# Normalising attention probabilities inside their transposing product

## The chip, the cores and the metric

The kernel runs on one core of a Trainium2 chip. The metric is the device time of one execution in microseconds; the time of the kernel before is the median of three runs. Each engine of the core (TensorE, here PE; VectorE, DVE; ScalarE, ACT; GpSimd, POOL; SyncE, SP) works through its own queue in order, and they wait for each other through semaphores. PEld is TensorE's loading of weights, which is recorded apart from its products. The rows come from one profiled execution.

## The reference

Two layers of a hybrid block over 512 latent tokens and 256 context tokens, 1024 wide. Each layer has a neighbourhood attention, a state-space mixer (SSD) and a grouped-query attention side by side, then a feed-forward part. The change touches only the softmax that both attentions use:

```python
def gqa_softmax_attention(q, k, v):
    s = jnp.einsum('bqgrd,bkgd->bgrqk', q, k) * (HEAD_DIM ** -0.5)
    p = jax.nn.softmax(s.astype(jnp.float32), axis=-1).astype(v.dtype)
    return jnp.einsum('bgrqk,bkgd->bqgrd', p, v)
```

Everything is float32. The neighbourhood attention has the same form, with a bias and a window mask added to `s`.

## The kernel before

The large projections (`proj_ws`, its product is L348, and `proj_as`, L362) split each float32 operand into a high and a low part of the type fp32r and add three products. They fill most of the span. The attention of a layer is a stage of its own between the input projections and the output projection: about 270 to 430 us in layer 0 and 1250 to 1385 us in layer 1.

Attention is cut into units. One unit is one head `j` of a pair, one block of 128 queries `qi`, and the 256, 640 or 768 keys that these queries see (2, 5 or 6 tiles of 128). Layer 0 has 48 units, layer 1 has 32; together they have 384 tiles. A unit goes through four steps:

- `scores` (L402, L405): two fp32r products into the PSUM tile `S`; DVE adds a bias where there is one and takes the row maximum (L410, L414, L415, or L419, L420); ACT writes the exponentials to the SBUF tile `pr` and, by the accumulator, their row sums (L422). Queries lie on the partitions, keys along the row.
- `normalise` (L426, L427): DVE takes the reciprocals of the 128 sums, then POOL multiplies the whole of `pr` by them, in place.
- `transposes` (L436): for each tile of 128 keys TensorE transposes 128x128 of `pr` into the PSUM tile `PT`, three tiles to a `PT`, and ACT (L440) or DVE (L442) copies them to `PHA` or `PHB`.
- `values` (L448): after both heads, TensorE multiplies the transposed probabilities by the values; both heads run side by side in the two halves of the array.

The loop that issues them (at the end of the mixer part) is software-pipelined by hand: in turn `i` it issues the scores of unit `i + 2`, then `normalise` of unit `i + 1`, then `transposes` of unit `i`, then `values` of the unit before. Between them a list of events with due times (`U = UCFG[l]`, L1101, and the lines behind it) spreads the work of the SSD mixer over the units: `diag` (row broadcasts by DMA; ACT L912 and L918; DVE L916, L923, L924, L931, L932, L940; POOL L927; TensorE L921, L937, L938), `steps` (POOL L963 and L1003; TensorE L982 and L995; DVE L977, L990, L1000), `skip` (POOL L944) and `gate` (DVE L1027, POOL L280). The biases of the neighbourhood attention are made on POOL too (L613). So in this stage all engines carry attention and mixer in one stream each.

The kernel is written on a layer that sets all waits and chooses tile buffers. It is called with a planner (`schedule_with_timeline_sim`, L1405), which sets the order of the instructions on each engine from the order of the program and its own estimate of their times. Tiles with one tag share a number of buffers: `pr` has three; `zt` has two of 128x256 floats and is used, ahead of attention, by the gate of the mixer (L810 to L814: two DVE or ACT steps, then a store to DRAM).

Of the kernel before, what the change touches and what calls it, by code (L numbers as in the profile page):

```python
# [11 lines left out]
ALU = mybir.AluOpType  # L12
AX = mybir.AxisListType

P = 128
# [13 lines left out]
def hybrid_kernel(ctx: ExitStack, tc: tile.TileContext, a, out, dbg=None):  # L29
# [4 lines left out]
    sb = ctx.enter_context(tc.tile_pool(name="sb", bufs=1))  # L34
# [5 lines left out]
    def nm(s):  # L40
        uid[0] += 1
        return f"{s}_{uid[0]}"

    def T(pool, tag, bufs, shape, dt=F32):
        return pool.tile(shape, dt, tag=tag, bufs=bufs, name=nm(tag))
# [7 lines left out]
    def slot(tag, dt=F32, shape=(P, NT)):  # L53
        return T(sb, tag, BUFS[tag], list(shape), dt)
# [16 lines left out]
    def tiny(n):  # L71
        if n <= 16:
            return T(sb, "tiny", 14, [P, n])
        return T(sb, "tiny36", 5, [P, n]) if n <= 36 else T(sb, "tiny96", 4, [P, n])

    def ps_s():
        return T(ps, "S", 2, [P, 1024])

    def ps_t():
        return T(ps, "PT", 2, [P, 512])  # L80

    def ps_sm():
        return T(ps, "sm", 2, [P, 512])
# [28 lines left out]
    V = nc.vector  # L112
    S = nc.scalar
    G = nc.gpsimd
    PE = nc.tensor
# [5 lines left out]
    ident = c0[:, 0:P]  # L121
# [265 lines left out]
    def attn(V2, xk, kts, qcols, bias, yout):  # L387


        nkt = len(kts)  # L390
        nk = nkt * P
        ng = (nkt + 2) // 3
        o0 = 512 - (xk[1] - xk[0]) if xk else 512
        ph, pr, t2, ms = {}, {}, {}, {}

        def scores(qk, j, qi):
            Q, K1, K2 = qk()
            q0 = qcols[qi]
            st = ps_s()
            for i, K in enumerate((K1, K2)):  # L400
                if xk:
                    PE.matmul(  # L402
                        st[:, o0:512], lhsT=Q[:, q0 : q0 + P], rhs=K[:, xk[0] : xk[1]], start=(i == 0), stop=(i == 1)
                    )
                PE.matmul(st[:, 512:768], lhsT=Q[:, q0 : q0 + P], rhs=K[:, 512:768], start=(i == 0), stop=(i == 1))  # L405
            m = ms[j, qi] = tiny(8)
            if bias is not None:
                if j not in t2:
                    t2[j] = bias(j)
                V.tensor_tensor_reduce(  # L410
                    out=st[:, o0:512], in0=st[:, o0:512], in1=t2[j][qi], scale=1.0, scalar=-3.0e38,
                    op0=ALU.add, op1=ALU.max, accum_out=m[:, 0:1],
                )
                V.tensor_reduce(out=m[:, 1:2], in_=st[:, 512:768], op=ALU.max, axis=AX.X)  # L414
                V.tensor_scalar(  # L415
                    out=m[:, 2:3], in0=m[:, 0:1], scalar1=m[:, 1:2], scalar2=-1.0, op0=ALU.max, op1=ALU.mult
                )
            else:
                V.tensor_reduce(out=m[:, 0:1], in_=st[:, o0:768], op=ALU.max, axis=AX.X)  # L419
                V.tensor_scalar_mul(m[:, 2:3], m[:, 0:1], -1.0)  # L420
            p_ = pr[j, qi] = T(sb, "pr", 3, [P, nk])
            exps.append(S.activation(p_, st[:, o0:768], AF.Exp, bias=m[:, 2:3], accum_out=m[:, 3:4]).ins)  # L422

        def normalise(j, qi):
            m, p_ = ms[j, qi], pr[j, qi]
            V.reciprocal(m[:, 4:5], m[:, 3:4])  # L426
            G.tensor_scalar(out=p_, in0=p_, scalar1=m[:, 4:5], scalar2=1.0, op0=ALU.mult, op1=ALU.mult)  # L427

        def transposes(j, qi):
            t_ = ph[j, qi] = slot("PH" + "AB"[j], F32, (P, 6, P))  # L430
            for i in range(ng):
                n = min(3, nkt - 3 * i)
                pt = ps_t()
                for k in range(n):
                    kk = 3 * i + k
                    PE.transpose(pt[:, k * P : (k + 1) * P], pr[j, qi][:, kk * P : (kk + 1) * P], ident)  # L436
                ptv = pt[:, 0 : n * P].rearrange("p (k q) -> p k q", q=P)
                dst = t_[:, 3 * i : 3 * i + n, :]
                if i % 2 == 0 or qi:
                    S.activation(dst, ptv, AF.Copy)  # L440
                else:
                    V.tensor_copy(dst, ptv)  # L442

        def values(qi):
            pv = ps_sm()
            for k in range(nkt):
                for j in range(2):
                    PE.matmul(  # L448
                        pv[64 * j : 64 * j + 64, 0:P], lhsT=V2(kts[k], j), rhs=ph[j, qi][:, k, :],
                        start=(k == 0), stop=(k == nkt - 1), tile_position=(0, 64 * j),  # L450
                    )
            yout(pv, qi)

        return [
            (lambda qk, j=j, qi=qi: scores(qk, j, qi), lambda j=j, qi=qi: normalise(j, qi),
             lambda j=j, qi=qi: transposes(j, qi), (lambda qi=qi: values(qi)) if j else None, j,
             (lambda j=j: t2.update({j: bias(j)})) if bias is not None and qi == 0 else None)
            for j in range(2) for qi in range(2)
        ]
# [46 lines left out]
    for l in range(L):  # L506
# [63 lines left out]
        for i in range(2, 4):  # L570
            step_md(4)
            w = wblk(i)
            pt = ps_s()
# [10 lines left out]
        for b in range(2):  # L584
            step_md(4)
            w = wv[b]
            pt = ps_s()
# [8 lines left out]
            for i in range(2):  # L596
                pt = ps_t()
# [20 lines left out]
        def na_sets():  # L618
            for b in range(2):
# [7 lines left out]
                for half in range(nhalf):  # L627
                    yt = []

                    def yout(pv, qi, b=b, half=half, yt=yt):  # L630
                        if qi == 0:
                            yt.append(sb_())
                        yv = yt[0]
                        if half < 2:
                            yv = yv.rearrange("p (r c) -> p r c", r=8)
                            ov = yv.rearrange("p r c -> p c r")[:, 16 * qi : 16 * qi + 16, :]
                            S.activation(ov, pv[:, 0:P].rearrange("p (c r) -> p c r", r=8), AF.Copy)
                            ydst = ydr[b][:, 0:512].rearrange("p (r c) -> p r c", c=64)[:, :, 32 * half : 32 * half + 32]
                        else:
                            S.activation(yv[:, qi * P : qi * P + P], pv[:, 0:P], AF.Copy)  # L640
                            ydst = ydr[b][:, 512:768]
                        if qi == 1:
                            nc.scalar.dma_start(ydst, yv)

                    if half < 2:
                        units += attn(
                            vsel, (128 * half, 128 * half + 384), [half, half + 1, half + 2, 4, 5],
                            [256 * half, 256 * half + 128], lambda j, b=b, half=half: na_bias(2 * b + j, half), yout,
                        )
                    else:  # L650
                        units += attn(vsel, None, [4, 5], [512, 640], None, yout)
# [72 lines left out]
        def gqa_sets():  # L724
            for g in range(2):
                def prep(g=g):
                    kk = prep_k(gqk[0], 64 * g)
                    return [(prep_q(gqk[1 + g], 64 * j, ntok), *kk) for j in range(2)]

                def vsel(kt, j, g=g):  # L730
                    return Vg[:, kt, 64 * g : 64 * g + 64]

                units = []
                for half in range(nhalf):
                    def yout(pv, qi, g=g, half=half):
                        k = 6 + g
                        if yh[k] is None:
                            yh[k], yl[k] = (mb([P, NT], F32R) if g else slot("GV", F32R) for _ in range(2))
                        o = 256 * half + P * qi
                        split(yh[k][:, o : o + P], yl[k][:, o : o + P], pv[:, 0:P])  # L740

                    if half < 2:
                        units += attn(vsel, (0, 512), list(range(6)), [256 * half, 256 * half + 128], None, yout)
                    else:
                        units += attn(vsel, None, [4, 5], [512, 640], None, yout)
                yield prep, units
# [261 lines left out]
        zt = []  # L1008
# [212 lines left out]
        for i, d in enumerate(dA):  # L1221
            events(nu + i)
            w = load_wo(d, 0)
            pt = ps_s()
# [5 lines left out]
        for d in range(KB - 2):  # L1230
            w = load_wo(d)
            pt = ps_s()
# [43 lines left out]
        for gi, ng in enumerate(groups):  # L1276
# [34 lines left out]
            for d in range(KB - 2 if fin else KB):  # L1311
                w = load_dn(d)
                pt = ps_s()
# [95 lines left out]
```

## Time and profile before

| | |
|---|---|
| median of 3 runs | 1808.84 us (1803.02 to 1810.6) |
| profiled execution | 1808.68 us, of which its span is 1806.9 us |
| TensorE busy | 1727.2 us (96%) |
| DVE busy | 1072.8 us (59%) |
| POOL busy | 395.0 us (22%) |
| mean granted TensorE clock | 0.978 of 2.4 GHz |

An engine's busy time is the union of its instructions' spans. TensorE's products overlap, and a product's recorded span includes the time that it takes to run out; so in a row of equal products the distance from start to start, not the duration of one, is what another product costs. The chain of waits follows the work that ended last back through what released it. Idle time is shown with the instruction that ended it.

### The profile page before, as it was taken

The page shows a single profiled execution, that of the slowest core. Times are in us where ns is not written, and L with a number is a line of the kernel's source. Part 1 is how long each engine was busy: PE and PEld are TensorE (multiplying, and loading weights), DVE is VectorE, ACT ScalarE, POOL GpSimd, SP SyncE. Part 2 cuts the span into 40 slices and gives each one's busy share as a digit, 9 for nine tenths or more (in the row PEclk, how much of TensorE's full clock was granted, in tenths as well). Part 3 has the DMA queues.
Part 4 walks back from the last instruction along what each step waited for, and adds up shares of the span by engine and source line. Part 5 has one row for each costly group of instructions (what it writes and reads, how often), then busy time and mean ns, then how long its engine had stood idle before and what let it go on. Part 6 is the DMA issues. An engine that isn't in the chain of part 4 may idle for free.

```text
span 1806.9 us, 26557 instructions
## 1 busy us (share of the span) xinstructions
PE 1727.2 (96%) x10146; PEld 1472.2 (81%) x10146; DVE 1072.8 (59%) x2141; ACT 682.5 (38%) x1376; POOL 395.0 (22%) x385
## 2 busy tenths in 40 slices
PE   7997798999999999999999999999899999999998
PEld 3887697777888888888888878988777888888887
DVE  4749957986575464445644576586886733333335
ACT  4564665665252211221122224333565532222222
POOL 0398876652010000000000001222652100000000
PEclk9999898999989999999999999999999999999999
DMA  9653474622224343334343445233622333333332
GB/s 363 204 167 98 129 236 130 165 87 65 71 70 138 108 120 124 107 104 121 116 124 117 123 155 180 84 99 114 186 71 71 90 105 93 96 101 94 95 109 78
DMA packets 94319, 221.66 MB, mean 123 GB/s; under 512 B 18416, under 2 KB 26224, under 8 KB 94192
## 3 DMA queue, kind: packets, MB, share of 16 engines
q1 hardware_dynamic: 78096, 204.65, 37.2%
q10 hardware_dynamic: 16096, 15.31, 2.5%
q8 instruction: 80, 1.31, 0.3%
q14 instruction: 47, 0.39, 0.1%
HBM read 198.49 MB, written 21.43 MB: 122 GB/s over the span
## 4 chain that ended last, share of the span: by engine, by line
PE 77%; DVE 11%; POOL 3%; DMA 3%; issue 3%; ACT 2%; ACTq 0%; SPq 0%; DVEq 0%; POOLq 0%
PE S L348 61%; PE sm L448 2%; PE PT L362 2%; PE PT L436 2%; PE PT L348 1%; PE sm L362 1%; DMA wr<-in_mod_wT_dram 1%; PE S L402 1%; POOL tiny L280 1%; DVE wh L916 1%; DVE pr L690 1%; PE S L405 1%; DVE wl L337 1%; POOL KA L239 1%; PE S L189 1%
## 5 line engine op out<-in xcount | busy, mean ns | idle before, releaser
L336 ACT ACTIVATE wh<-wr 128x1024 fp32r<-128x1024 f32 (+2 forms) x204 | 198.0, 972 | 711.3 <-PE S L348 542.6
L337 DVE TENSOR_TENSOR wl<-wr,wh 128x1024 fp32r<-128x1024 f32 (+2 forms) x204 | 233.7, 1147 | 179.3 <-ACT wh L336 177.0
L280 POOL TENSOR_TENSOR tiny<-tiny,mhalf 128x2 f32<-128x2 f32 (+2 forms) x17 | 27.6, 1623 | 1072.2 <-DVE tiny L1198 1022.9
L348 PE MATMUL S<-HY,wh 128*128 128x512 f32 (+1 forms) x716 | 213.7, 356 | 5.4 <-ACT HY L329 4.1
L348 PE MATMUL S<-HY,wl 128*128 128x512 f32 (+1 forms) x716 | 213.5, 355 | 0.0
L348 PE MATMUL S<-HZ,wh 128*128 128x512 f32 (+1 forms) x716 | 211.9, 354 | 0.4 <-DVE HZ L330 0.4
L348 PE MATMUL S<-HS,wl 128*128 128x512 f32 (+1 forms) x716 | 212.2, 354 | 0.0
L348 PE MATMUL S<-HS,wh 128*128 128x512 f32 (+1 forms) x716 | 210.6, 352 | 0.0
L242 DVE CUSTOM_DVE_ANT_0 PT<-wr,XFB 128x512 f32<-128x512 f32 x112 | 75.6, 715 | 181.6 <-DMA wr<-in_mod_wT_dram 181.6
L348 PEld LDWEIGHTS S<-HY,wh 128*128 128x128 f32 x716 | 119.1, 191 | 25.6 <-ACT HY L329 4.3
L348 PEld LDWEIGHTS S<-HS,wh 128*128 128x128 f32 x716 | 118.2, 190 | 20.0
L348 PEld LDWEIGHTS S<-HZ,wh 128*128 128x128 f32 x716 | 117.5, 190 | 20.3 <-DVE HZ L330 1.3
L348 PEld LDWEIGHTS S<-HY,wl 128*128 128x128 f32 x716 | 118.3, 190 | 18.6
L348 PEld LDWEIGHTS S<-HS,wl 128*128 128x128 f32 x716 | 117.6, 190 | 18.3
L348 PE MATMUL S<-PHA,wh 128*128 128x512 f32 (+1 forms) x358 | 106.2, 354 | 0.0
L348 PE MATMUL S<-PHB,wh 128*128 128x512 f32 (+1 forms) x358 | 105.0, 351 | 0.0
L348 PE MATMUL S<-GX,wh 128*128 128x512 f32 (+1 forms) x400 | 98.1, 351 | 0.4 <-DVE KA L1152 0.4
L427 POOL TENSOR_SCALAR pr<-pr,tiny 128x640 f32<-128x640 f32 (+2 forms) x80 | 73.5, 922 | 67.6 <-DVE tiny L426 56.1
L1299 DVE TENSOR_TENSOR MB<-S,MA 128x768 f32<-128x768 f32 (+1 forms) x42 | 34.6, 823 | 71.3 <-PE S L348 71.2
L436 PE MATMUL PT<-c,pr 128*128 128x128 f32 x384 | 65.6, 285 | 11.1 <-POOL pr L427 5.2
L239 POOL TENSOR_TENSOR KA<-QN,XFB 128x512 f32<-128x512 f32 x48 | 66.7, 1394 | 41.7 <-ACT XFB L216 22.9
L348 PEld LDWEIGHTS S<-GX,wh 128*128 128x128 f32 x400 | 66.1, 189 | 11.6 <-DVE KA L1152 0.8
(432 smaller groups left out, 3895.6 us busy)
## 6 DMA issues: line engine op xcount, KB each, us to landing
wr<-in_mod_wT_dram SPq DMA_DIRECT2D x56, 512.0 KB, 3.8
wr<-in_w_gate_dram SPq DMA_DIRECT2D x44, 512.0 KB, 3.6
wr<-in_w_up_dram SPq DMA_DIRECT2D x44, 512.0 KB, 3.6
wr<-in_w_blk_dram SPq DMA_DIRECT2D x28, 512.0 KB, 3.8
wr<-in_w_down_dram SPq DMA_DIRECT2D x32, 448.0 KB, 3.3
QN<-in_mod_wT_dram SPq DMA_DIRECT2D x48, 256.0 KB, 2.9
wr<-in_w_out_dram SPq DMA_DIRECT2D x32, 256.0 KB, 2.7
wr<-in_w_down_dram SPq DMA_DIRECT2D x16, 512.0 KB, 3.6
```

What stands on the lines that cost most here:

```text
L189: PE.matmul(pm[32 * j : 32 * j + 32, 0:512], lhsT=cs[:, k, :], rhs=w[k], start=(k < 4), stop=(k >= 4), tile_position=(0, 32 * j),)
L239: G.tensor_tensor(out=p_, in0=wv, in1=x, op=ALU.mult)
L242: V.tensor_tensor_reduce(out=p_, in0=wv, in1=x, scale=1.0, scalar=0.0, op0=ALU.mult, op1=ALU.add, accum_out=acc[:, o : o + 1],)
L280: POW.tensor_tensor(out=y, in0=v, in1=mhalf[:, 0:n], op=ALU.pow)
L336: S.activation(hi, raw, AF.Copy)
L337: V.tensor_tensor(lo, raw, hi.bitcast(F32), ALU.subtract)
L348: ins = PE.matmul(pt[:, c0:c1], lhsT=w, rhs=xx[:, c0:c1], start=(k == (0 if len(order) == 1 else order[0]) and i == 0), stop=(k == (nk - 1 ...
L362: PE.matmul(pt[:, 0:n], lhsT=s, rhs=w[:, o : o + n], start=(k == 0 and i == 0), stop=(k == KB - 1 and i == 2),)
L427: G.tensor_scalar(out=p_, in0=p_, scalar1=m[:, 4:5], scalar2=1.0, op0=ALU.mult, op1=ALU.mult)
L436: PE.transpose(pt[:, k * P : (k + 1) * P], pr[j, qi][:, kk * P : (kk + 1) * P], ident)
L448: PE.matmul(pv[64 * j : 64 * j + 64, 0:P], lhsT=V2(kts[k], j), rhs=ph[j, qi][:, k, :], start=(k == 0), stop=(k == nkt - 1), tile_position= ...
L1299: V.tensor_tensor(gg[:, c0:c1], pu[:, c0:c1], sg[:, c0:c1], ALU.mult)
```

## The change

`normalise` no longer multiplies `pr`. It makes, on DVE, a 128x128 diagonal matrix from the identity and the reciprocals. There is one tile `dg[j]` of two such matrices for each head, in the two buffers of the tag `zt`. `transposes` multiplies the unnormalised `pr` tile, as the stationary operand, by that diagonal instead of calling the transposition with the identity; the product is an ordinary float32 matrix product into the same `PT`.

```diff
-        ph, pr, t2, ms = {}, {}, {}, {}
+        ph, pr, t2, ms, dg = {}, {}, {}, {}, {}
...
         def normalise(j, qi):
-            m, p_ = ms[j, qi], pr[j, qi]
+            m = ms[j, qi]
             V.reciprocal(m[:, 4:5], m[:, 3:4])
-            G.tensor_scalar(out=p_, in0=p_, scalar1=m[:, 4:5], scalar2=1.0, op0=ALU.mult, op1=ALU.mult)
+            if qi == 0:
+                dg[j] = T(sb, "zt", 2, [P, 2, P])
+            V.tensor_scalar_mul(dg[j][:, qi, :], ident, m[:, 4:5])
...
-                    PE.transpose(pt[:, k * P : (k + 1) * P], pr[j, qi][:, kk * P : (kk + 1) * P], ident)
+                    PE.matmul(
+                        pt[:, k * P : (k + 1) * P], lhsT=pr[j, qi][:, kk * P : (kk + 1) * P], rhs=dg[j][:, qi, :],
+                        start=True, stop=True,
+                    )
```

## Rows read from the trace of the kernel before

**Rows 1.** The page: busy time, share of the span, instructions of three engines.

```profile
PE 1727.2 (96%) x10146; PEld 1472.2 (81%) x10146; DVE 1072.8 (59%) x2141; ACT 682.5 (38%) x1376; POOL 395.0 (22%) x385
```

**Rows 2.** The page: the chain that ended last, shares of the span by engine.

```profile
PE 77%; DVE 11%; POOL 3%; DMA 3%; issue 3%; ACT 2%; ACTq 0%; SPq 0%; DVEq 0%; POOLq 0%
```

**Rows 3.** Busy time by stretch: both attention stages, all engines; the columns are named.

```profile
core 0: us, PE busy (x) PEld busy (x) DVE busy (x) ACT busy (x) POOL busy (x), PEclk, DMA share, GB/s
270.00:420.00 150.00, 138.50 (x1039) 112.33 (x1038) 126.69 (x350) 91.34 (x246) 91.50 (x115) 0.97 0.42 118
1250.00:1385.00 135.00, 124.89 (x960) 100.86 (x958) 104.22 (x272) 77.30 (x200) 76.55 (x91) 0.99 0.41 115
...
sum 285.00, PE 263.39 PEld 213.18 DVE 230.91 ACT 168.64 POOL 168.05; mean PE 131.69 PEld 106.59 DVE 115.45 ACT 84.32 POOL 84.03
```

**Rows 4.** The chain by line, shares: first 265 to 430, then 1250 to 1390 us.

```profile
by line: PE sm L448 12.3%; PE PT L436 8.1%; PE S L402 6.6%; PE S L405 5.9%; issue 5.8%; PE S L348 5.6%; PE PT L982 4.3%; ACT pr L422 4.3%; DVE wh L916 4.2%; PE PT L995 3.4%; PE sm L938 3.2%; DVE tiny L419 3.1%; PE sm L937 3.1%; DVE HY L1027
...
by line: PE sm L448 15.1%; PE PT L436 10.4%; PE S L348 7.3%; DVE wh L916 6.0%; PE S L402 5.8%; DVE tiny L419 4.0%; PE sm L362 3.8%; PE PT L982 3.7%; PE sm L937 3.4%; DMA GR<-in_rpb_dram 3.4%; PE PT L995 3.3%; PE sm L938 3.2%; issue 3.1%; PE
```

**Rows 5.** The chain's pieces: start, us, what; DVE's first and last, then POOL's.

```profile
273.95 0.57 DVE S L410
...
1384.39 0.76 DVE KA L1152
...
353.56 1.83 POOL HY L1003 x2
...
1268.42 1.34 POOL pr L427
1293.94 0.80 POOL pr L427
```

**Rows 6.** Groups by form: xcount, busy us, mean ns, idle before, what ended it.

```profile
L436 PE MATMUL PT<-c,pr 128*128 128x128 f32 x384 | 65.6, 285 | 11.1 <-POOL pr L427 5.2 <-ACT PHA L440 1.4 <-POOL XFB L963 1.0
L921 PE MATMUL sm<-GC,GT 128*128 128x128 f32 x40 | 8.3, 290 | 0.0
L982 PE MATMUL PT<-XFB,GB 128*128 128x256 f32 x80 | 22.1, 400 | 0.9 <-ACT PHA L440 0.6 <-ACT PHB L440 0.4
```

**Rows 7.** Timeline near 372 us: start, us, engine, line, tiles, shape, records.

```profile
371.52 0.82 PE L436 MATMUL PT<-c,pr 128*128 128x128 f32 x6
...
372.64 0.49 PE L921 MATMUL sm<-GC,GT 128*128 128x128 f32 x2
...
373.67 1.02 PE L982 MATMUL PT<-XFB,GB 128*128 128x256 f32 x4
```

**Rows 8.** Groups by form on DVE: three kinds of small float32 work.

```profile
L916 DVE SCALAR_TENSOR_TENSOR wh<-wh,dtr,wl 128x128 f32<-128x128 f32 x80 | 40.2, 539 | 0.6 <-ACT wl L912 0.2
...
L415 DVE TENSOR_SCALAR tiny<-tiny 128x1 f32<-128x1 f32 x32 | 6.5, 203 | 0.2
L835 DVE TENSOR_SCALAR tiny<-tiny 128x96 f32<-128x96 f32 x14 | 5.8, 411 | 0.3
...
L832 DVE TENSOR_SCALAR tiny<-tiny 128x96 f32<-128x96 f32 x2 | 0.4, 206 | 0.0
```

**Rows 9.** Timeline from 140.8 us: one DVE step and the POOL step beside it.

```profile
141.25 0.98 DVE L835 TENSOR_SCALAR tiny<-tiny 128x96 f32<-128x96 f32 x1
...
140.84 1.32 POOL L239 TENSOR_TENSOR KA<-QN,XFB 128x512 f32<-128x512 f32 x1 [1.55 <-ACT KA L240]
```

**Rows 10.** Busy time of L427 alone in both stages, summed.

```profile
sum 285.00, POOL 70.53; mean POOL 35.26
```

**Rows 11.** Who waited for whom, whole span: us in total, times, longest.

```profile
POOL pr L427 <- DVE tiny L426: 56.1, 23, 24.5
POOL HY L1003 <- DVE tiny L426: 15.7, 6, 5.3
...
PE PT L436 <- POOL pr L427: 5.2, 6, 2.1
```

## The prediction

> **What bounds the kernel now.** I read the page first. TensorE is busy 96% of the span, DVE 59%, POOL 22% [rows 1], and the chain of waits runs over PE for 77% of the span and over POOL for 3% [rows 2]. That speaks of a kernel bound by TensorE, but it is an average: the change lives in the two attention stages alone, so the next view is the busy time by stretch, for these stages. There PE is busy 263.4 of 285 us, DVE 230.9 and POOL 168.1 [rows 3]. DVE, a bystander in the whole, is at 81% here (126.69 of 150 us, 84%, in layer 0), so two engines are nearly full, and a third is well used. The reader should see that nobody has a reserve of 40 us in this stage except POOL and ACT.
>
> Next I read the chain for these two stretches by line. L436, the transposes, is its second line with 8.1% of 165 us and 10.4% of 140 us, which makes 13.4 + 14.6 = 28 us [rows 4]. Adding up DVE's pieces of the same chain (105 pieces in layer 0 and 76 in layer 1, of which the first and the last stand there) gives 43 + 33 = 76 us, a quarter of the 305 us [rows 5]. POOL's pieces add up to about 11 us, among them only two of L427, 2.1 us together; most of the rest is L1003, L927, L963 and L613 [rows 5]. Last I read who waits for the step that goes away: TensorE's transposes waited for L427 six times, 5.2 us in all, out of 80 units [rows 11]. So the in-place multiply on POOL is almost always hidden: the scores run two units ahead of the transposes.
>
> **Part 1: POOL's multiply goes.** It is 70.5 us of POOL's work in the stages [rows 10]. What lies on the chain of it is 2.1 us. There is also an indirect part: POOL's queue is in order, so while L427 waits for the reciprocal (56.1 us, 23 times) the mixer's L1003, L927 and L963 stand behind it, and L1003 is shown with another 15.7 us that ended on the reciprocal's semaphore [rows 11]. Mixer steps on POOL come forward, and of the some 9 us of other POOL pieces on the chain I take 4 as regained; the bounds are 0 and 9. Together -6 us, bounds -2 and -11. The reciprocal itself (L426) stays where it was.
>
> **Part 2: a transposition becomes a float32 product.** This is the largest term. A transposition of 128x128 is one record: 384 records for 384 tiles [rows 6], and six in a row take 0.82 us with a single one lasting 0.27, so (0.82 - 0.27) / 5 = 0.11 us from one to the next [rows 7]. The trace has an ordinary float32 product of exactly the new shape: L921, 128x128 by 128x128. The code issues 20 of them (one for each of 12 + 8 chunk-and-group pairs), and there are 40 records [rows 6]: each product is two records. What a record costs is seen better at L982, whose two products of 256 columns are four records in 1.02 us: (1.02 - 0.38) / 3 = 0.213 us for 256 columns [rows 7], 0.107 us for 128. L921 agrees: 0.49 - 0.275 = 0.215 us from its first to its second record includes the load of the first weights [rows 7]. So a tile goes from 0.11 to 2 x 0.107 = 0.213 us, and 384 tiles add 384 x 0.107 = 41 us of array time, at the 2.4 GHz level; the granted clock of the stages is 0.97 and 0.99 of that [rows 3].
>
> How much of the 41 us lands on the end? The transposes' array time is 384 x 0.11 = 42 us, and they hold 28 us of the chain, two thirds. Two thirds of 41 us is 27; as the 28 us also contain the run-out of each group of two or three, which isn't doubled, I take 25. The other third runs where PE waits for somebody else: PE has 285 - 263.4 = 21.6 us of recorded idle time in the stages [rows 3], enough for 16 us if it falls well. The bounds of this term are 8 us (all idle time, and some run-out, absorbs the rest) and 41 us (none of it does).
>
> The Trainium skill prices it differently. "TensorE: Matmul & The Clock Gate", section Terms, calls the transposing mode four times faster for FP32, and "FP8 and Floating Point Precision", section TensorE Precision Notes, gives true FP32 four passes. The rows here don't agree with a factor of four between the two: it is two records against one, with an equal 0.107 to 0.11 us each.
>
> **Part 3: DVE makes a diagonal, 80 times.** No row shows a DVE multiply of 128x128 SBUF floats by a column of scalars. The nearest are L832, 128x96 with constants, 206 ns undisturbed; L415, whose scalar is a column in SBUF, 203 ns for a single element; and from above L916 of the right shape with two tensors, 539 ns in the mean of all [rows 8]. I take 0.28 us, nearest to L832 with more columns and the fetch of the column; the bounds are 0.21 and 0.54. To that comes a wait: L835, the same kind of step as L832 in the same shape, has a mean of 411 ns [rows 8], and where a two-input POOL step ran beside it, it took 0.98 us and ended together with that step [rows 9]. With L427 gone, POOL is still busy for (168.1 - 70.5) / 285 = 34% of the stages, with steps of some 0.6 to 0.8 us, so on average about 0.34 x 0.35 = 0.12 us of waiting. That is 0.40 us a unit and 80 x 0.40 = 32 us more DVE work, which lifts DVE from 81 to about 89% of a stage lengthened by a tenth. A quarter of the chain in the stages is DVE, so 8 us of it on the path; bounds 4 and 20, as DVE's own share of the chain grows. What is queued behind this step on DVE is the mixer's L916 to L940 and the next unit's row maximum (L419, L414), and for that ACT's exponentials wait.
>
> The Trainium skill has a rule here that speaks against moving the work to DVE: "SBUF — State Buffer", section Who interferes with whom, says that a DVE step in a two-port mode, tensor_scalar among them, and a GpSimd step block each other for the whole instruction. The trace agrees, with the 0.98 us beside the 0.206.
>
> **Part 4: waits.** The transposes now wait for the diagonal instead of POOL. From the reciprocal that is 0.4 us instead of about 0.9 plus POOL's queue, so this wait gets shorter; the 5.2 us were counted in part 1. The buffers of `zt` are free in time: `dg[j]` is needed again four units later. Only at the start of a stage does the first one follow the mixer's gate, whose store must have landed, and in layer 1 the second `dg` can fall on the buffer of the first and wait for the transposes of unit 1. That is one wait in a layer of at most a group or two, under 2 us; I take 0.
>
> **Sum.** -6 + 25 + 8 = +27 us on the profiled execution's 1808.7 us (1806.9 of span and 1.8 around it): 1835.7. The median of the runs is 1808.84, equal to it within 0.2 us, so the forecast is 1836 us.
>
> **The rivals.** (a) TensorE and DVE bind throughout: all 41 us of products land on the path, DVE's 8 too, and POOL gives back nothing. 1808.7 + 49 = 1858 us. For it: PE is at 92% and DVE at 81% in the stages. Against it: a third of the transposes is off the chain today. (b) The products fall into waiting time: the array is idle at the ends of groups where PE waits for ACT's copies and DVE, and the second record of a product hides there; 8 us of products, 8 of DVE, -8 of POOL: 1817 us or below, down to 1810; this can't be told from no change in its lower half. For it: 21.6 us of idle PE and 11 us of idle time ahead of L436 alone [rows 6]. Against it: L436's share of the chain. (c) Faster: POOL's queue is the hidden bound. If L427's waits hold up L1003, L927 and L963, and through them DVE and PE, POOL's whole 11 us leave the chain, and the 5.2 us of the transposes with them; with only 8 us paid for products and 4 for DVE this gives 1808.7 - 16 + 12 = 1805 us, and down to 1797 if DVE's steps are all off the path and the products cost no more than 4 us. It decides from the point where PE's extra stays under 12 us. For it: 56 us of POOL's queue standing still [rows 11]. Against it: POOL has only some 11 us on the chain. (d) A product takes four times a transposition, as the pages of the Trainium skill named above would have it (by that rule): 0.33 us more for each, 125 us more, 83 of it on the path at the same two thirds: about 1894 us. The records of L921 and L982 speak against it. (e) The change doesn't do what it says, as a product with a diagonal is still one record: then only -6 + 8, 1811 us; L921 speaks against it.
>
> **How the numbers follow.** The forecast with its spread of 10 us either way has 0.60, (a) 0.17, (b) 0.13, (c) 0.05, (d) 0.03, (e) 0.02. The range from 1814 to 1860 leaves out (c), (d), (e) and a part of (b), together about 0.16. A difference of 0.5%, 9 us, is about what a measurement of this kernel can tell from no change; slower by more than that means above 1817.9 us. Slower has the forecast, (a), (d) and a small part of (b): 0.83. Within 0.5% are most of (b), (e) and half of (c): 0.14. Faster by over 0.5% has 0.03.
>
> **What would show it.** L436 should have 768 records instead of 384, and six tiles in a row should take about 1.4 us instead of 0.82. L427 should be gone, and POOL's busy time in the stages about 98 us. DVE should show 80 new steps with a median near 0.28 us and a tail up to 1 us beside POOL's steps. The stages should be longer by some 15 us each, the rest of the span unchanged, and L436's share of the chain should be near 16%. The prediction is wrong if the stages grow by less than 4 us each (then idle time took the products, or POOL's queue did matter), if a tile is not two records of 0.107 us, or if time changes outside of the stages, which would mean that the planner set another order there.

## The result and the profile after

| | before | changed |
|---|---|---|
| median of 4 runs | 1808.64 us | 1831.6 us (1829.46 to 1835.98) |
| ratio | | 1.0146, 95% interval 1.0126 to 1.0167 |
| profiled execution | 1808.68 us, span 1806.9 | 1830.35 us, span 1828.6 |

The change makes the kernel slower, by 23 us by the medians and by 26 us (23 to 30) by the ratio; the forecast was 27 us, 1836 us, with a range of 1814 to 1860.

The changed kernel's page, parts 1 and 4 (busy time, and the chain by engine), answers to [rows 1, 2]:

```profile
PE 1760.8 (96%) x10530; PEld 1514.3 (83%) x10530; DVE 1089.2 (60%) x2221; ACT 685.1 (37%) x1376; POOL 319.3 (17%) x305
...
PE 79%; DVE 11%; DMA 3%; POOL 3%; issue 2%; ACT 2%; SPq 0%; ACTq 0%; DVEq 0%; POOLq 0%
```

A record is one instruction of an engine in the profile. TensorE's records grew by 384, from 10146 to 10530, POOL lost its 80 instructions and 75.7 us, DVE gained 80. PE's busy time grew by 33.6 us, and its idle time in the span fell from 79.7 to 67.8 us, by 11.9: 33.6 - 11.9 = 21.7 us, the growth of the span. So of the 41 us of array time that were added some 12 filled idle time. Where the remaining 7 us went is told further down (the clock).

The groups by form of the new work, to be read against L436 in [rows 6]:

```profile
L438 PE MATMUL PT<-zt,pr 128*128 128x128 f32 x768 | 112.7, 285 | 5.3 <-DVE zt L429 2.0 <-DVE PHB L447 1.4 <-ACT PHB L445 0.9
...
L429 DVE TENSOR_SCALAR zt<-c,tiny 128x128 f32<-128x128 f32 x80 | 35.1, 439 | 3.4 <-DMA zsp<-zt 1.8 <-PE PT L438 0.3
```

There are two records for each tile, 768. The timeline of the changed kernel beside [rows 7] shows that each costs what a transposition cost:

```profile
367.92 1.60 PE L438 MATMUL PT<-zt,pr 128*128 128x128 f32 x12
370.06 1.50 PE L438 MATMUL PT<-zt,pr 128*128 128x128 f32 x12
```

Six tiles are twelve records. With the 0.27 us of a single one taken off, the second run gives (1.50 - 0.27) / 11 = 0.112 us a record, the first 0.121; six transpositions took 0.82 us.

Where in the span the time went is read from lines that stand ahead of and behind the two attention stages: the exponentials of the decays (L843 before, L848 after; first and last start belong to layer 0 and layer 1) and the feed-forward part (L1299, L1304). The columns are min/median/max duration and first and last start. First the kernel before, then the changed one:

```profile
L843 ACT ACTIVATE EX<-sm x2: 558/565/572, 221.2 to 1193.5; 128x480 f32<-128x480 f32 x2
...
L1299 DVE TENSOR_TENSOR MB<-S,MA x42: 690/820/958, 553.2 to 1757.0; 128x768 f32<-128x768 f32 x21, 128x512 f32<-128x512 f32 x21
```

```profile
L848 ACT ACTIVATE EX<-sm x2: 559/566/572, 218.9 to 1205.2; 128x480 f32<-128x480 f32 x2
...
L1304 DVE TENSOR_TENSOR MB<-S,MA x42: 691/822/958, 564.5 to 1778.7; 128x768 f32<-128x768 f32 x21, 128x512 f32<-128x512 f32 x21
```

The changed kernel is 2.3 us ahead before the first stage, 11.3 us behind after it, 11.7 us behind before the second, and 21.7 us behind after that. The stretches with the stages took 13.6 and 10.0 us more; the rest of the span stayed within 2.3 us. A lead of that size ahead of the first stage says nothing about the change: the twelve profiles of this document reach this point between 217.1 and 225.9 us.

The chain by line, over the lengthened stages (265 to 445 and 1262 to 1412 us), answers to [rows 4]:

```profile
by line: PE PT L438 20.2%; PE sm L453 15.4%; PE S L402 5.4%; PE S L348 5.2%; PE sm L942 5.1%; PE S L405 5.0%; PE sm L943 4.9%; issue 4.9%; PE PT L1000 4.6%; PE PT L987 4.4%; DVE wh L921 3.7%; DVE tiny L419 2.4%; DVE zt L429 2.0%; DMA GR<-in
...
by line: PE PT L438 25.5%; PE sm L453 16.0%; PE S L402 7.9%; PE S L348 7.3%; DVE wh L921 4.7%; PE PT L987 4.2%; PE PT L1000 4.2%; PE S L405 3.8%; PE sm L943 3.6%; PE sm L942 3.6%; PE sm L362 3.3%; DVE zt L429 2.1%; PE PT L362 1.9%; issue 1.
```

L438 holds 0.202 x 180 + 0.255 x 150 = 75 us of the chain, 47 more than L436 held and more than the 41 us of array time that were added: products that were hidden as transpositions are on it now. Adding up the listed pieces of the chain in these stages by engine (the shortest are not listed), PE went from 174 to 253 us, DVE from 76 to 51, ACT from 20 to 6, POOL from 11 to 3. The path didn't get longer by the products alone; it moved from DVE, ACT and POOL to TensorE.

### The profile page after: what moved, and what is told of

Read it like the earlier page. It is cut to its first block, busy times and chain, and to the rows that moved or that the text cites. A ratio compares the mean times of both kernels' runs of the same rounds, so it can differ in the third digit from the quotient of the medians.

```text
span 1828.6 us, 27262 instructions
## 1 busy us (share of the span) xinstructions
PE 1760.8 (96%) x10530; PEld 1514.3 (83%) x10530; DVE 1089.2 (60%) x2221; ACT 685.1 (37%) x1376; POOL 319.3 (17%) x305
## 4 chain that ended last, share of the span: by engine, by line
PE 79%; DVE 11%; DMA 3%; POOL 3%; issue 2%; ACT 2%; SPq 0%; ACTq 0%; DVEq 0%; POOLq 0%
PE S L348 59%; PE PT L438 4%; PE sm L453 3%; DMA wr<-in_mod_wT_dram 2%; PE PT L362 2%; PE PT L348 1%; PE sm L362 1%; PE S L402 1%; DVE wl L337 1%; POOL tiny L280 1%; PE S L405 1%; PE sm L942 1%; PE PT L1000 1%; PE sm L943 1%; PE PT L987 1%
## 5 line engine op out<-in xcount | busy, mean ns | idle before, releaser
L438 PE MATMUL PT<-zt,pr 128*128 128x128 f32 x768 | 112.7, 285 | 5.3 <-DVE zt L429 2.0
L438 PEld LDWEIGHTS PT<-zt,pr 128*128 128x128 f32 x768 | 97.3, 193 | 16.2 <-issue 3.9
L1304 DVE TENSOR_TENSOR MB<-S,MA 128x768 f32<-128x768 f32 (+1 forms) x42 | 34.6, 823 | 70.7 <-PE S L348 70.5
```

The lines of the kernel that those rows point to most:

```text
L438: PE.matmul(pt[:, k * P : (k + 1) * P], lhsT=pr[j, qi][:, kk * P : (kk + 1) * P], rhs=dg[j][:, qi, :], start=True, stop=True,)
L1304: V.tensor_tensor(gg[:, c0:c1], pu[:, c0:c1], sg[:, c0:c1], ALU.mult)
```

## The experiments

The change has three parts: the product (P), the diagonal on DVE (D), and POOL's multiply gone (G). Five kernels with some of the parts say what each is worth; five more ask why the product costs what it does. Ratios are against the kernel before on the same chip; a difference in us is the ratio's on 1808.6 us. It isn't the time less 1808.6: on the chips of the experiments the kernel before has medians of 1803.9 to 1806.8 us, and the ratio isn't the quotient of the medians, which would give 27 us for the product alone where the ratio gives 31. The difference between two of the kernels is uncertain by 6 to 9 us. "Clock" is the mean granted clock of 280 to 425 and of 1270 to 1380 us, stretches that lie inside both stages in each kernel but the one with the product twice, whose second stretch is 1310 to 1450 us; each comes from one profiled execution.

| kernel | parts | ratio (95% interval) | difference | clock |
|---|---|---|---|---|
| before | none | 1 | 0 | 0.95, 0.98 |
| no POOL multiply | G | 0.9989 (0.9967 to 1.0010) | -2 us | 0.95, 0.98 |
| diagonal only | D | 1.0086 (1.0054 to 1.0119) | +16 us | 0.95, 1.00 |
| all but the product | D, G | 1.0041 (1.0018 to 1.0064) | +7 us | 0.92, 0.94 |
| product only | P | 1.0169 (1.0137 to 1.0202) | +31 us | 0.98, 1.00 |
| product, no POOL | P, G | 1.0126 (1.0092 to 1.0161) | +23 us | 1.00, 1.00 |
| the change | P, D, G | 1.0146 (1.0126 to 1.0167) | +26 us | 0.99, 1.00 |
| transposed twice | 2 transpositions | 1.0127 (1.0090 to 1.0164) | +23 us | 0.99, 1.00 |
| product twice | 2 x P, D, G | 1.0600 (1.0559 to 1.0642) | +109 us | 1.00, 1.00 |
| product in fp32r | P in 1 record, D, G | 1.0048 (1.0026 to 1.0070) | +9 us | 0.87, 0.97 |
| fp32r, diagonal on POOL | the same, D on POOL | 1.0048 (1.0022 to 1.0073) | +9 us | 0.88, 0.94 |
| diagonal on ACT | P, G, D on ACT | 1.0144 (1.0107 to 1.0181) | +26 us | 1.00, 1.00 |

**The product alone.** On the kernel before:

```diff
-                    PE.transpose(pt[:, k * P : (k + 1) * P], pr[j, qi][:, kk * P : (kk + 1) * P], ident)
+                    PE.matmul(
+                        pt[:, k * P : (k + 1) * P], lhsT=pr[j, qi][:, kk * P : (kk + 1) * P], rhs=ident,
+                        start=True, stop=True,
+                    )
```

> Only the product is taken over: the tile of pr is multiplied by the identity as an ordinary float32 product, POOL still multiplies by the reciprocals, DVE makes no diagonal. Additive theory (the prediction's sum): product alone +25 us on 1808.6, so 1834 us. Rival (with the products TensorE sets the pace of the stages alone, whatever DVE and POOL do): the same as the changed kernel, 1831.6 us, within 2 us. Clock: if the products keep the clock up, reduced-clock time in the two stages is about 3.4 us as in the changed kernel, if it was chance it lies anywhere up to the 17 us of before.

1833.62 us, +31 us with an interval of 25 to 37. Both readings were near this, so it doesn't tell them apart by itself; it shows that the product by itself costs as much as the whole change.

**No multiply on POOL.**

```diff
-            G.tensor_scalar(out=p_, in0=p_, scalar1=m[:, 4:5], scalar2=1.0, op0=ALU.mult, op1=ALU.mult)
```

> The transpositions of before, and no normalisation at all: POOL's multiply is left out (the output is then not divided by the sums). Additive theory: -6 us, 1803 us. Rival of a hidden bound in POOL's queue: -16 us or more, 1793 us or below. Clock: about 17 us of reduced clock in the stages if transpositions let it fall.

1803.44 us, -2 us (-6 to +2). The rival of a hidden bound in POOL's queue falls: taking 70 us of work from POOL is worth 2 us, not 16, although L427 and the mixer's steps behind it stood waiting for over 70 us [rows 11].

**The product, without POOL's multiply and without the diagonal** (both edits above).

> The products, with the identity in place of the diagonal, no diagonal on DVE and no multiply on POOL (the normalisation is left out). Against the changed kernel this takes away DVE's 80 steps alone. Additive theory: 8 us below the changed kernel, 1824 us. Rival (TensorE sets the pace): within 2 us of the changed kernel, 1830 to 1833 us.

1826.62 us, +23 us (17 to 29). Against the product alone, removing POOL's multiply gives 8 us here (-1 to 16), against 2 before. Against the change, removing the 80 DVE steps gives 4 to 5 us (-4 to 11), between the two theories. Neither can be told from nothing by these runs.

**All but the product.** The change, with the transposition by `ident` kept; nothing reads `dg`.

> All of the change but the product: POOL's multiply is gone, DVE makes the diagonals, but the transpositions of before still use the identity, so nothing reads the diagonals (the normalisation is left out). Additive theory: -6 + 8 = +2 us, 1811 us. Rival: with transpositions DVE is as much a bound as TensorE, so the diagonals cost their whole 35 us at DVE's share of the path or more, 1815 us and above.

1814.94 us, +7 us (3 to 12), 9 us (4 to 15) above the kernel without POOL's multiply. The steps themselves took 393 ns in the mean:

```profile
L429 DVE TENSOR_SCALAR zt<-c,tiny 128x128 f32<-128x128 f32 x80 | 31.3, 393 | 2.4 <-DMA zsp<-zt 1.8
```

**The diagonal only**, with POOL's multiply and the transposition kept (the three added lines of `normalise` put behind POOL's multiply).

> The kernel before, to which DVE adds the 80 diagonals that nothing reads; POOL's multiply and the transpositions stay. Additive theory: +8 us, 1814 us. If POOL's in-place multiply holds DVE's steps up as its two-input steps do, the mean of the 80 steps is well above the 0.44 us of the changed kernel and the time 1820 us or more.

1821.39 us, +16 us (10 to 22). The mean of a step is 570 ns:

```profile
L430 DVE TENSOR_SCALAR zt<-c,tiny 128x128 f32<-128x128 f32 x80 | 45.5, 570 | 2.4 <-DMA zsp<-zt 1.8
```

So the second reading holds for the steps: the same 80 take 31 us beside a POOL without L427 and 45 us beside one with it. The change takes away a part of what hinders the step that it adds. In time they cost 9 and 16 us, on the same side, but these intervals overlap.

**Transposed twice.** The kernel before, with `for _ in range(2):` ahead of the transposition.

> The kernel before with every transposition issued twice into the same PSUM tile: two records for each tile as with the products, but in transposing mode. If the cost is the array time of the second record: 384 x 0.11 = 42 us more array time, the same +27 us as the product alone, 1834 us. If it is a load on TensorE that keeps the clock up, the two stages show 0 to 7 us of reduced clock, as the three kernels with products did (0, 3.4, 6.8). If transpositions don't count for the clock, as the Trainium skill has it (TensorE: Matmul & The Clock Gate, Part 4: PE-mode transpose), the stages show 17 us or more (as the three kernels with transpositions did: 17, 17, 37), and the time is 5 us or more above that of the product alone.

1831.31 us, +23 us (16 to 30): within the error what the product costs, alone or with the rest. The cost is the second record of 0.11 us, whatever it computes. The clock is told below.

**The product twice.** The changed kernel, with `for _ in range(2):` ahead of the product.

> The changed kernel with every product issued twice, four records for each tile: another 82 us of array time. If two thirds of TensorE's work in the stages stay on the path: 55 us above the changed kernel, 1886 us. If with the products the stages are bound by TensorE alone: the whole 82 us, 1913 us.

1915.88 us; the ratio to the changed kernel is 1.0600 / 1.0146, +82 us on 1831.6. The second reading holds: the second 82 us of array time land whole on the end (73 to 90); of the first 41 only 19 to 31 did. By the chain, L439 (the product's line in this kernel) now holds 39.2% of 265 to 490 us:

```profile
by line: PE PT L439 39.2%; PE sm L454 14.2%; PE S L348 5.8%; PE S L402 5.6%; PE S L405 5.1%; PE PT L1001 4.2%; PE sm L944 4.0%; PE sm L943 4.0%; PE PT L988 3.4%; DMA HZ<-zsp 2.7%; issue 2.0%; DVE MB L775 1.3%; PE sm L927 1.2%; DVE S L410 1.
```

**The product in fp32r.** On the changed kernel:

```diff
-            p_ = pr[j, qi] = T(sb, "pr", 3, [P, nk])
+            p_ = pr[j, qi] = T(sb, "pr", 3, [P, nk], F32R)
...
-                dg[j] = T(sb, "zt", 2, [P, 2, P])
+                dg[j] = T(sb, "zt", 2, [P, 2, P], F32R)
```

> The changed kernel with pr and the diagonal in the type fp32r, so that the product takes one record instead of two (less exact). If the two records are what the change costs: one record of at most 0.107 us, so TensorE has the array time of before, and the time falls by the product's 25 us to 1807 us, or a little above the 1806.75 of before by the diagonals' 4 to 9 us: 1807 to 1815. If the cost lies in waiting for the diagonals: no fall, 1828 us or above. If a record of 128 columns takes half of 0.107 us: below the kernel before, 1795 us.

1815.39 us, +9 us (5 to 13). The product is one record now, and 18 of the 26 us are gone, as the first reading had it. What is left, 9 us, is within the error the 7 us of the kernel with all but the product. The group and a run of six tiles in this kernel:

```profile
L438 PE MATMUL PT<-zt,pr 128*128 128x128 f32 x384 | 68.5, 293 | 7.3 <-ACT PHA L445 3.5 <-DVE zt L429 2.4 <-ACT HS L993 0.6
...
369.45 0.78 PE L438 MATMUL PT<-zt,pr 128*128 128x128 f32 x6
```

(0.78 - 0.27) / 5 = 0.10 us: no cheaper than a transposition, so there is nothing here to beat the kernel before with.

**The diagonal on ACT.** On the changed kernel:

```diff
-            V.tensor_scalar_mul(dg[j][:, qi, :], ident, m[:, 4:5])
+            S.activation(dg[j][:, qi, :], ident, AF.Copy, scale=m[:, 4:5])
```

> The changed kernel with the diagonals made on ACT (a copy with the reciprocals as its scale) instead of DVE. ACT has 40% of the stages free; its step of this shape, L912, takes 0.39 us. If DVE's 80 steps cost 4 to 9 us on the path: 1823 to 1828 us. If they are hidden behind TensorE: 1831 us, or more if ACT's exponentials get late.

1835.49 us, ratio 1.0144 beside the change's 1.0146. Taking 35 us from DVE gave nothing; the step took 398 ns on ACT:

```profile
L429 ACT ACTIVATE zt<-c,tiny 128x128 f32<-128x128 f32 x80 | 31.5, 398 | 13.1 <-DVE tiny L426 12.5 <-DVE tiny L420 0.6
```

Either DVE's steps are worth little beside the products, or ACT lost by them what DVE won; this run can't tell which.

**fp32r with the diagonal on POOL**, the candidate for a version as fast as before:

```diff
-            V.tensor_scalar_mul(dg[j][:, qi, :], ident, m[:, 4:5])
+            G.tensor_scalar(out=dg[j][:, qi, :], in0=ident, scalar1=m[:, 4:5], scalar2=1.0, op0=ALU.mult, op1=ALU.mult)
```

> The fp32r product (one record for each tile) with the diagonals made on POOL, 128x128 each in place of the whole of pr: neither TensorE's second record nor DVE's 80 steps, and a fifth of POOL's former work. Additive theory: the kernel without POOL's multiply, 0 to 6 us below before, 1800 to 1806 us, which no measurement here tells from before. If an fp32r product lets the clock fall more than a transposition (44 us of reduced clock in the stages of the fp32r kernel with DVE's diagonals): still 1812 us or above, and over 30 us of reduced clock. If it was DVE's steps that let TensorE starve there: 17 us of reduced clock or less.

1813.94 us, +9 us (4 to 13): the additive theory fails here by some 9 us, although DVE has no added steps. In their place TensorE now waits for POOL's diagonals, 10.9 us in 14 places, two thirds of it weight loads, against 3.5 us in 5 for DVE's, so this run doesn't price DVE's steps. The reduced clock in the two stages adds up to 48 us, 31 more than before, which at half the speed is worth some 15 us. No version was found that beats the kernel before, and leaving POOL's whole multiply out is worth 2 us, 6 at the most.

## The clock in the stages

No term of the forecast has this. The kernel before spends 17 us of its two stages at the lower level of the clock (1.2 GHz), the changed kernel 3.4 us. The stretches by busy time, granted clock in the third column from the end; first the kernel before:

```profile
280.00:425.00 145.00, 135.44 (x1016) 109.09 (x1017) 123.07 (x344) 91.01 (x249) 88.39 (x109) 0.95 0.43 121
1270.00:1380.00 110.00, 104.28 (x802) 83.17 (x801) 89.90 (x227) 64.91 (x165) 64.22 (x76) 0.98 0.40 112
```

The changed kernel:

```profile
280.00:425.00 145.00, 139.31 (x1101) 119.45 (x1099) 123.44 (x361) 84.92 (x231) 43.41 (x58) 0.99 0.39 113
1270.00:1380.00 110.00, 107.55 (x856) 92.82 (x856) 95.79 (x254) 62.16 (x153) 37.96 (x50) 1.00 0.45 127
```

All but the product:

```profile
280.00:425.00 145.00, 129.28 (x953) 107.86 (x953) 126.49 (x373) 87.65 (x240) 50.00 (x68) 0.92 0.40 117
1270.00:1380.00 110.00, 101.00 (x746) 83.14 (x746) 98.12 (x266) 65.10 (x163) 37.85 (x51) 0.94 0.48 130
```

Transposed twice:

```profile
280.00:425.00 145.00, 139.18 (x1114) 117.37 (x1115) 120.45 (x325) 87.17 (x236) 81.30 (x106) 0.99 0.41 116
1270.00:1380.00 110.00, 107.25 (x864) 90.49 (x863) 92.35 (x227) 63.08 (x155) 63.65 (x78) 1.00 0.46 128
```

The product in fp32r:

```profile
280.00:425.00 145.00, 131.17 (x915) 111.50 (x915) 124.00 (x364) 87.74 (x236) 48.02 (x62) 0.87 0.40 117
1270.00:1380.00 110.00, 103.44 (x784) 86.12 (x782) 97.37 (x274) 66.27 (x168) 39.46 (x53) 0.97 0.47 133
```

Adding up the record of the granted clock over both stages, the six kernels with one record for each tile were at the lower level for 17, 17, 17, 37, 44 and 48 us (before, no POOL multiply, diagonal only, all but the product, the two in fp32r), and the six with two or more for 0 to 6.8 us. Each figure is from one profile, but the clock of whole executions, which is on record for every run, agrees in the mean: 0.980 to 0.981 for the kernel before, 0.979 to 0.980 for the two kernels with only the diagonal or only POOL's multiply gone, 0.972 to 0.975 for the other three with one record, 0.981 to 0.985 for the six with two or more, of which the product alone, at 0.981, is hardly above the kernel before. The kind of instruction doesn't decide it: transpositions issued twice keep the clock as products do, and with the diagonals in place of POOL's multiply single transpositions (0.9745 over 11 runs) lose it as single fp32r products do (0.9739 over 11). Two records a tile instead of one go with the higher clock. Among the kernels with one, TensorE's busy time doesn't order them: with the same 238 us of it in these stretches the kernel without POOL's multiply was at the lower level for 17 us, and the fp32r kernel with POOL's diagonals for 48. "TensorE: Matmul & The Clock Gate" of the Trainium skill, section Part 4: PE-mode transpose, says that the full clock doesn't engage for the transposing mode; the kernel that transposes twice, with 0.99 and 1.00 and twelve records in a row in 1.53 us, 0.115 us each, disagrees for float32.

The clock also tells two kinds of loss apart. Take the stretches from L843 to the first and last step of L1299 in its form `MB<-PT` (221.2 to 539.1 and 1193.5 to 1451.7 us before, the same lines in the others). The two fp32r kernels are 9 and 10 us longer there than the kernel before, with TensorE's idle time the same within 0.3 us: what they lose shows as busy time at the lower clock. The kernel with the diagonal only is 15.6 us longer, of which 13.7 us are idle time: it loses by waiting.

For the balance: 13.6 us less at the lower level are 6.8 us of array time. 41 us added, less 6.8, is 34 us, and PE's busy time grew by 33.6; less 11.9 us of idle time that was filled, it is the 21.7 us of the span. That is a balance from one profile of each kernel, and the clock differs outside of the stages too (0.978 and 0.986 over the span), so the 6.8 us are shown as an order of size, not to the microsecond. The product's three prices further down go the same way, by single profiles: where it brought 10, 17 and 34 us back from the lower level, it cost 31, 25 and 19 us.

## Why the prediction was right, point by point

**The product (forecast +25, bounds 8 and 41).** Its size was right: two records of 0.11 us, 768 in all, six tiles in 1.50 us where 1.4 was said. Its share on the path was right in size too: 31 us on the kernel before; 25 us on the kernel without POOL's multiply (1.0126 against 0.9989); 19 us on the one with everything else (1.0146 against 1.0041). The reason given was only half right. The forecast had a third of the products off the path, behind TensorE's idle time, and the products at about 16% of the chain; L438 holds 20 and 25%, 75 us of their 768 x 0.11 = 84. What paid for the missing 16 us was idle time that was filled, 12 us, and a clock that fell less, about 7 us, which the forecast didn't have. That two thirds of 41 us came out is luck in this part.

**The diagonal (forecast +8, bounds 4 and 20).** 0.28 us undisturbed and 0.12 of waiting were forecast; the median is 286 ns, the mean 439, the longest 1542 (min/median/max):

```profile
L429 DVE TENSOR_SCALAR zt<-c,tiny x80: 267/286/1542, 275.9 to 1391.6; 128x128 f32<-128x128 f32 x80
```

Beside a POOL step it waits as L835 did in [rows 9]; here in the changed kernel, DVE's step and POOL's bias step, which end together:

```profile
287.67 1.05 DVE L429 TENSOR_SCALAR zt<-c,tiny 128x128 f32<-128x128 f32 x1
```

```profile
287.12 1.53 POOL L618 TENSOR_TENSOR GR<-GR,c 128x768 f32<-128x768 f32 x1
```

Its price came out at 16 us with POOL's multiply still there, 9 without it, 4 to 5 beside the products. The sum's 8 was for the last of these; on the changed kernel's chain L429 holds 2.0 and 2.1%, 7 us, and the runs don't show that 8 was too much. The 89% of DVE's time that was given for the lengthened stage isn't what its own terms make, (230.9 + 32) / 313 = 84%, and 81% was measured from 270 to 433 and 1262 to 1405 us; nothing in the sum hangs on it.

**POOL's multiply (forecast -6, bounds -2 and -11).** 2 us on the kernel before (-2 to 6), 8 us once the products are there (-1 to 16). The forecast took one number for both, and its 6 lies at the end of the first interval and inside the second.

**The waits.** The price of 0 for the `zt` buffers holds: L429 waited 1.8 us once for the mixer's store and 0.3 us once for L438, both at the start of layer 1. TensorE waited 2.0 us in three places for the diagonal, where it had waited 5.2 us in six for POOL.

**The rivals.** (a), with 1858 us, is refuted by the measured 1831.6; but it describes what comes next, as doubling the product showed with 82 us for 82. (b) falls by the product alone; idle time took 12 us and not 33. (c) falls by the kernel without POOL's multiply, -2 us. (d) and (e) fall by the 768 records of 0.11 us.

**The places.** 15 us a stage were forecast, 13.6 and 10.0 measured, and the rest of the span unchanged but for 2.3 us, so an order set anew by the planner elsewhere played no part that these profiles show.

**The sum.** The kernel got slower by the path that was named, and inside the range; that -6 + 25 + 8 came within a microsecond of the ratio's 26 is luck. Each measured alone on the kernel before, the three parts give 31 + 16 - 2 = 45 us, 36 to 54 with their errors: they don't add up. The forecast's terms were near to what the parts cost in each other's company, for the product by another mechanism than the one given.

## What to carry to other kernels

A step that is hidden on a free engine is worth what the chain shows of it, here 2 us for 70 us of work; moving it into the busiest engine costs that engine's whole added time, less the idle time that it fills and, here, less what a higher clock gives back. Count the records of an instruction of the same type and shape before putting it in place of a transposition: here it was two instead of one. And the terms of such a sum are worth different amounts in different company (together 45 us alone, 26 in the change), so an effect that is measured alone isn't what it will be in the whole change.

## What wasn't expected of the hardware

The granted clock of a stage with TensorE 92% busy [rows 3] still falls for 17 us, and adding 41 us of work to TensorE keeps it up; taking a record away again, as the fp32r products did, lets it fall for 44 to 48 us, 27 to 31 more than before, which at half the speed takes back some 14 to 15 us of what was won. The kernel with all but the product, with single transpositions, lost 37 us, so it isn't the type of the product. Why the clock falls so much more when the diagonals stand in place of POOL's multiply than with either of these edits alone (37 to 48 us against 17) is left open. A float32 product's record and an fp32r product's record of 128 columns cost the same 0.10 to 0.11 us here.
